# A two-layer transformer trunk on one core: the feed-forward as seven block products on fp32 sums, in two stages with DRAM between them

## The chip, the cores and the metric

The kernel runs on one core of a Trainium2 chip. The metric is device microseconds of one execution. The program uses four compute engines with a queue each, which run in order and wait for each other by semaphores: TensorE (PE: matmuls and transposes into PSUM), VectorE (DVE), ScalarE (ACT) and GpSimd (POOL). SyncE (SP) issues the DMAs. On-chip data lies in SBUF (128 partitions) and in PSUM, whose eight banks hold 128 x 512 fp32 each.

## The reference

The input x has 1024 tokens of 1024 features, all in fp32, and goes through two layers. In short:

```
for layer in range(2):
    mix = mixer(x)                      # layer 0: latent attention and sliding window; layer 1: forgetting and chunked attention
    x = layer_norm(alpha * x + mix, ln1)            # alpha = (2 * 2) ** 0.25
    g = x @ w_gate ; u = x @ w_up                   # 1024 -> 2816
    ffn = (silu(g) * u) @ w_down                    # 2816 -> 1024
    x = layer_norm(alpha * x + ffn, ln2)
```

## The kernel before

**Precision.** TensorE multiplies in a reduced fp32 form (F32R in the code). To keep fp32 accuracy each operand is split in a high part (a cast on ScalarE, L106, or L116 for weights) and a low part (operand minus high part, on VectorE, L107, or for weights on GpSimd, L117). A product is then three matmuls, high by high, high by low and low by high, summed in one PSUM bank (`mm3`, L127). The unit of work is a matmul of 128 x 128 by 128 x 512.

**Order of the work.** The code is written with pools of tiles and handed to a scheduler, which estimates times and puts the instructions of each engine in a fixed queue. What an instruction writes is a tile of a pool (names: g, h, s, t, b and wh/wr in SBUF; pd, ps, pt, pv in PSUM). It can start when the tile's former user is done. So a queue's order is known before the run, and an instruction that waits holds up all that is behind it in its queue.

**One layer.** The mixer writes its heads to DRAM (`o_scr`). `out_proj` reads them back and projects them in two halves of the sum. As each tile of 128 tokens is done, it goes through LN1 in `ln_pipe`: statistics on VectorE (L153), small operations on GpSimd (L144, L146), the normalisation on ScalarE (L163), the gain on GpSimd (L164), the bias on VectorE (L192). `ln_turn` (L172 and the splits at L106 and L107) transposes the tile and puts its high and low parts in `xt`, the transposed activations.

**Feed-forward** (`swiglu_ln`). The 2816 hidden features are 22 tiles f of 128. They are worked through in groups of two (the last of four). For each f, gate and up are computed for two halves of 512 tokens, as `h = silu(g) * u` in 128 features x 1024 tokens. For f = 0 and 1 all is plain: 96 matmuls per f. For f = 2 to 19 the cross terms (high by low, low by high) of part of the sum go through block sums in `gate_up`, in seven instead of eight block products: 90 matmuls. For f = 20 and 21 fewer blocks do so: 92. The sums of weights for this are made by GpSimd (L223). After each group, the group's share of the down product, with each tile's two halves of 512 output features, is added to y in SBUF (L363, L365). In the last group `push` starts LN2 for each tile as it is complete. LN2's transposes (layer 0) feed layer 1. In layer 1, tokens 768 to 1023 of LN2 are normalised by VectorE alone (L200), in halves.

Of the kernel before, what the change touches and what calls it, by code (L numbers as in the profile page):

```python
# [11 lines left out]
F32 = mybir.dt.float32  # L12
# [6 lines left out]
S = 1024  # L19
# [13 lines left out]
CFG = dict(gp=33, wrp=3, whp=5, sp=3, hp=3, bp=2, tp=2, pd=3, ps=2, pt=2, pv=1)  # L33
# [6 lines left out]
class Core:  # L40
# [43 lines left out]
    def t(self, tag="t"):  # L84
        return self.tp.tile([P, 512], F32, tag=tag, bufs=3 if tag == "dt" else 2, name=self.nm("t"))
# [23 lines left out]
    def weight(self, src, cols, hl=None):  # L109
        raw = self.wrp.tile([P, WC], F32, tag="wr", name=self.nm("wr"))[:, 0:cols]  # L110
        if hl is None:
            hl = self.whp.tile([P, 2, WC], F32R, tag="wh", name=self.nm("wh"))
# [12 lines left out]
    def mm3(self, out, stat, mov, first, last):  # L125
        for i, (a, c) in enumerate(((0, 0), (0, 1), (1, 0))):
            self.nc.tensor.matmul(out, stat[a], mov[c], start=first and i == 0, stop=last and i == 2)  # L127
# [50 lines left out]
    def ln_pipe(self, y, g, b, xt, done):  # L178
# [41 lines left out]
    def winograd(self, r, b):  # L220

        for i, (x, z, op) in enumerate(b):
            self.nc.gpsimd.tensor_tensor(r[i], fv(x), fv(r[z] if isinstance(z, int) else z), op=op)  # L223

    def sums_x(self, xt):

        def sums(r, b):
            self.winograd(r, ((b(0, 1), b(0, 0), ALU.subtract), (b(1, 1), 0, ALU.subtract),
                              (b(1, 1), b(0, 1), ALU.subtract), (b(1, 0), 1, ALU.subtract)))

        pair = "p (k c) -> p k c"
# [11 lines left out]
    def sums_w(self, wg, wu, more):
        def sums(r, k):
            self.winograd(r, ((k(wu, 0), k(wu, 1), ALU.add), (r[0], k(wg, 0), ALU.subtract),
                              (k(wg, 0), k(wu, 0), ALU.subtract), (k(wg, 1), 1, ALU.subtract)))

        s = [x for _ in range(2) for x in self.b().bitcast(F32R).rearrange("p (s l c) -> s p l c", s=2, l=2)]
        sums(s, lambda w, i: w[0][:, :, i * 256 : i * 256 + 256])
        r = [[x[:, 0, 0:P], x[:, 1, 0:P], x[:, 0, P:256], x[:, 1, P:256]] for x in s]  # L250
        if more:
            for l, tag in enumerate(("t", "o")):
                e = list(self.t(tag).bitcast(F32R).rearrange("p (s c) -> s p c", s=4))
                sums(e, lambda w, i: w[1][:, l, i * P : i * P + P])
                for i in range(4):
                    r[i].append(e[i])
        return r

    def cross(self, out, w, x, first, last):

        for i, (a, b) in enumerate(zip(w, x)):
            self.nc.tensor.matmul(out, a, b, start=first and i == 0, stop=last and i == len(w) - 1)  # L262

    def gate_up(self, wg, wu, xt, xs, more):


        nc = self.nc
        ss = self.sums_w(wg, wu, more)
        deep = 6 if more else 4
        tiles = ((0, 1, 4), (2, 3, 5))  # L270

        def blk(w, i):
            return [w[k // 4][:, l, k % 4 * P : k % 4 * P + P] for k in tiles[i] if k < deep for l in range(2)]

        def orig(i, half):
            return [self.feat(xt, k, half)[1 - l] for k in tiles[i] if k < deep for l in range(2)]

        def part(w, half, extra):
            p = self.psd()
            for k in range(KT):  # L280
                hl = w[k // 4]
                c = slice((k % 4) * P, (k % 4) * P + P)
                hi, lo = self.feat(xt, k, half)
                for i, (a, x) in enumerate(((0, hi), (0, lo), (1, hi))[0 : 1 if k < deep else 3]):
                    nc.tensor.matmul(p, hl[:, a, c], x, start=k + i == 0, stop=extra is None and k == KT - 1 and i == 2)  # L285
            if extra is not None:
                self.cross(p, *extra, False, True)
            return p

        def single(p, w, x):  # L290
            self.cross(p, w, x, True, True)
            return p
# [947 lines left out]
```

## Time and profile before

| | |
|---|---|
| median of 3 runs | 2534.13 us (2533.58 to 2534.38) |
| profiled execution | 2534.4 us |
| its span in the trace | 2532.6 us |
| mean granted TensorE clock | 0.99 |
| busy: PE, DVE, ACT, POOL | 2452.3, 1358.9, 970.8, 1365.9 us |
| matmul instructions (transposes included) | 12376 |

The span runs from the first to the last instruction in the trace. Busy time is the union of an engine's instructions, including the time in which one is held up after it started. The chain of waits is followed back from the last instruction: its shares tell how much of the span each engine decides. The granted clock is TensorE's clock as a share of its full 2.4 GHz.

### The profile page before, as it was taken

The page shows a single profiled execution, that of the slowest core. Times are in us where ns is not written, and L with a number is a line of the kernel's source. Part 1 is how long each engine was busy: PE and PEld are TensorE (multiplying, and loading weights), DVE is VectorE, ACT ScalarE, POOL GpSimd, SP SyncE. Part 2 cuts the span into 40 slices and gives each one's busy share as a digit, 9 for nine tenths or more (in the row PEclk, how much of TensorE's full clock was granted, in tenths as well). Part 3 has the DMA queues.
Part 4 walks back from the last instruction along what each step waited for, and adds up shares of the span by engine and source line. Part 5 has one row for each costly group of instructions (what it writes and reads, how often), then busy time and mean ns, then how long its engine had stood idle before and what let it go on. Part 6 is the DMA issues. An engine that isn't in the chain of part 4 may idle for free.

```text
span 2532.6 us, 35601 instructions
## 1 busy us (share of the span) xinstructions
PE 2452.3 (97%) x12376; PEld 2067.3 (82%) x12376; DVE 1358.9 (54%) x3096; ACT 970.8 (38%) x2112; POOL 1365.9 (54%) x1604
## 2 busy tenths in 40 slices
PE   8998999999999999999999999999899999999997
PEld 7976888788888888887789898977788888888886
DVE  3477757734444444447356666656724444444447
ACT  5475857422222222223356665555421222222221
POOL 3432545785555555566356553364685555555565
PEclk9999999999999999999999999999999999999999
DMA  4235331111111111112221212142111111111112
GB/s 153 79 101 167 92 119 50 52 51 50 50 50 50 51 50 50 50 55 105 71 78 59 68 45 65 41 154 74 42 44 50 50 51 50 50 50 50 51 57 97
DMA packets 103923, 172.66 MB, mean 68 GB/s; under 512 B 12728, under 2 KB 38712, under 8 KB 103744
## 3 DMA queue, kind: packets, MB, share of 16 engines
q1 hardware_dynamic: 103744, 170.39, 22.5%
q8 instruction: 98, 1.61, 0.3%
q14 instruction: 81, 0.66, 0.1%
HBM read 143.57 MB, written 22.58 MB: 66 GB/s over the span
## 4 chain that ended last, share of the span: by engine, by line
PE 85%; DVE 5%; POOL 3%; DMA 3%; ACT 2%; issue 2%; SPq 0%; POOLq 0%; DVEq 0%; ACTq 0%
PE pd L127 24%; PE ps L127 19%; PE pd L285 17%; PE pd L262 6%; PE pt L262 6%; PE pv L562 4%; PE pt L551 3%; PE pv L262 2%; POOL g L164 1%; PE ps L591 1%; PE ps L592 1%; DVE g L192 1%; DVE m L162 1%; DMA wr<-o_scr 1%; ACT g L163 1%
## 5 line engine op out<-in xcount | busy, mean ns | idle before, releaser
L117 POOL TENSOR_TENSOR wh<-wr,wh 128x512 fp32r<-128x512 f32 (+2 forms) x363 | 482.3, 1337 | 666.9 <-ACT wh L116 637.1
L127 PE MATMUL pd<-g,wh 128*128 128x512 f32 (+1 forms) x2076 | 530.9, 401 | 19.2 <-ACT g L106 10.1
L116 ACT CAST wh<-wr 128x512 fp32r<-128x512 f32 (+2 forms) x363 | 222.2, 613 | 748.6 <-PE pd L285 439.3
L285 PE MATMUL pd<-g,wh 128*128 128x512 f32 x1984 | 501.8, 389 | 0.0
L127 PEld LDWEIGHTS pd<-g,wh 128*128 128x128 f32 (+1 forms) x2076 | 382.7, 189 | 103.8 <-ACT g L106 11.0
L127 PE MATMUL ps<-wh,h 128*128 128x512 f32 x1920 | 460.9, 390 | 1.0 <-DVE g L365 1.0
L285 PEld LDWEIGHTS pd<-g,wh 128*128 128x128 f32 x1984 | 372.4, 188 | 77.3
L127 PEld LDWEIGHTS ps<-wh,h 128*128 128x128 f32 x1920 | 359.5, 188 | 77.4 <-DVE g L365 3.2
L365 DVE TENSOR_TENSOR g<-ps,g 128x512 f32<-128x512 f32 x288 | 197.0, 688 | 320.3 <-PE ps L127 320.3
L534 POOL TENSOR_SCALAR s<-s,m 128x128 f32<-128x128 f32 (+1 forms) x192 | 138.1, 720 | 174.0 <-DVE m L533 147.8
L107 DVE TENSOR_TENSOR h<-pt,h 128x512 fp32r<-128x512 f32 (+3 forms) x318 | 170.0, 543 | 47.3 <-ACT h L106 45.5
L106 ACT CAST h<-pt 128x512 fp32r<-128x512 f32 (+3 forms) x318 | 145.5, 472 | 119.2 <-PE pt L551 111.4
L562 PE MATMUL pv<-h,g 128*128 128x256 f32 x928 | 160.8, 295 | 5.2 <-ACT h L106 4.3
L529 ACT ACTIVATE s<-s,m 128x128 f32<-128x128 f32 (+1 forms) x192 | 143.9, 750 | 43.8 <-DVE m L527 37.7
L127 PE MATMUL pd<-wh,g 128*128 128x256 f32 (+2 forms) x1056 | 158.9, 296 | 0.8 <-DVE t L967 0.6
L127 PEld LDWEIGHTS pd<-wh,g 128*128 128x128 f32 x1056 | 145.2, 194 | 3.5 <-PE pt L939 0.8
L296 DVE TENSOR_TENSOR t<-pd,t 128x512 f32<-128x512 f32 x160 | 106.8, 686 | 72.7 <-PE pd L262 63.3
L562 PEld LDWEIGHTS pv<-h,g 128*128 128x128 f32 x928 | 129.4, 190 | 13.7 <-ACT h L106 6.6
L551 PE MATMUL pt<-ident,s 128*128 128x128 f32 x816 | 133.4, 274 | 6.5 <-DVE h L107 3.8
L296 DVE TENSOR_TENSOR t<-pt,t 128x512 f32<-128x512 f32 x80 | 55.3, 692 | 152.2 <-PE pt L262 150.3
L551 PEld LDWEIGHTS pt<-ident,s 128*128 128x128 f32 x816 | 98.5, 141 | 20.3 <-issue 6.1
L262 PE MATMUL pt<-g,b 128*128 128x512 f32 x320 | 105.0, 389 | 0.0
(192 smaller groups left out, 3798.9 us busy)
## 6 DMA issues: line engine op xcount, KB each, us to landing
wr<-in_wgu SPq DMA_DIRECT2D x176, 256.0 KB, 2.7
wr<-in_wd SPq DMA_DIRECT2D x88, 256.0 KB, 2.6
o_scr<-t SPq DMA_DIRECT2D x128, 64.0 KB, 2.1
wr<-o_scr SPq DMA_DIRECT2D x32, 256.0 KB, 2.8
wr<-in_cd_f SPq DMA_DIRECT2D x32, 256.0 KB, 2.7
s<-in_xT SPq DMA_DIRECT2D x16, 256.0 KB, 5.1
g<-qr_scr SPq DMA_DIRECT2D x32, 128.0 KB, 3.3
g<-kr_scr SPq DMA_DIRECT2D x16, 256.0 KB, 4.2
```

The source lines that it names most:

```text
L106: self.nc.scalar.copy(hi, src)
L107: self.nc.vector.tensor_tensor(lo, src, fv(hi), op=ALU.subtract)
L116: self.nc.scalar.copy(hl[:, 0, :], raw)
L117: self.nc.gpsimd.tensor_tensor(hl[:, 1, :], raw, fv(hl[:, 0, :]), op=ALU.subtract)
L127: self.nc.tensor.matmul(out, stat[a], mov[c], start=first and i == 0, stop=last and i == 2)
L262: self.nc.tensor.matmul(out, a, b, start=first and i == 0, stop=last and i == len(w) - 1)
L285: nc.tensor.matmul(p, hl[:, a, c], x, start=k + i == 0, stop=extra is None and k == KT - 1 and i == 2)
L296: nc.vector.tensor_tensor(o, x, z, op=ALU.add)
L365: nc.vector.tensor_tensor(y[tt][:, o], p, y[tt][:, o], op=ALU.add)
L529: nc.scalar.activation(sb[:, 0:w], sb[:, 0:w], AF.Exp, bias=neg, scale=scale, accum_out=sm)
L551: nc.tensor.transpose(tp[:, (kb - b0) * P : (kb - b0) * P + P], sb[:, (kb - k0) * P : (kb - k0) * P + P], self.ident)
L562: nc.tensor.matmul(pv, vt(kb), pair[kb // 4][:, l, kb % 4, :], start=c == 0, stop=c == 2 * (last + 1 - first) - 1)
```

## The change

**Blocks.** The feed-forward's products are cut in 2 x 2 blocks and computed with seven instead of eight block products (Winograd's form), now on sums of the fp32 values; each sum is split in a high and a low part afterwards, and all three matmuls of a product work on the split sums.

**Gate/up** (`gate_up`). The blocks are the two halves of the tokens, the two halves of the 1024 input features, and gate against up. `turn_sums` takes the place of `ln_turn` after LN1. For tokens 0 to 511 it transposes the tile as before. For tokens 512 to 1023 it makes four sums of 512 columns out of two tiles (two on VectorE, two on GpSimd) and transposes them beside the tile's second half. Per f, four sums of weights are made on GpSimd, and all weights and sums are split by ScalarE and VectorE (`hilo`). One f is 7 x 4 x 3 = 84 matmuls. h is written to DRAM (`h_scr`), and the LN1 output to `xr_scr`.

**Down** (`down`). It runs after all of gate/up. The blocks are the two halves of the tokens, the two halves of the output features, and f = j against f = j + 11. Both h and the weights come from DRAM in one tile of 1024 columns: 512 of h, 512 of weights. The pairs j are worked through in three groups of 3, 4 and 4; y is loaded from `xr_scr` again and multiplied by alpha. A group has seven products on 4 tiles of 128 tokens, and per j 12 matmuls for each product. The sums of h and of weights are made by GpSimd, two by VectorE, each operand is split by ScalarE and VectorE right ahead of its matmuls, and the results are added to y by VectorE and, for u, by GpSimd too.

**Pools.** The h tiles go from three of 2 x 1024 columns to six of 1024, the t tags become one tag with nine tiles, the g pool has 31 instead of 33 tiles, whp six instead of five. In the attention code only the tile names change by this.

```diff
-CFG = dict(gp=33, wrp=3, whp=5, sp=3, hp=3, bp=2, tp=2, pd=3, ps=2, pt=2, pv=1)
+CFG = dict(gp=31, wrp=3, whp=6, sp=3, hp=6, bp=2, tp=9, pd=3, ps=2, pt=2, pv=1)
...
+    def turn_block(self, xb, name, src, tt):
+        p = self.pst()
+        for k in range(4):
+            self.nc.tensor.transpose(p[:, k * P : k * P + P], src[:, k * P : k * P + P], self.ident)
+        o = slice(tt % 4 * P, tt % 4 * P + P)
+        hi, lo = self.block(xb, name)
+        for k in range(2):
+            self.split(hi[k][:, :, o], lo[k][:, :, o], p[:, k * 256 : k * 256 + 256].rearrange("p (k c) -> p k c", k=2))
+    def turn_sums(self, y, xb):
+        nc = self.nc
+        def turn(tt):
+            a, b = slice(0, 512), slice(512, D)
+            if tt < 4:
+                self.turn_block(xb, "b11", y[tt][:, a], tt)
+                self.turn_block(xb, "b21", y[tt][:, b], tt)
+                return
+            x, z = y[tt - 4], y[tt]
+            t1, t2, t3, t4 = (self.t() for _ in range(4))
+            nc.vector.tensor_tensor(t1, z[:, a], x[:, a], op=ALU.subtract)
+            nc.gpsimd.tensor_tensor(t3, z[:, b], z[:, a], op=ALU.subtract)
+            nc.vector.tensor_tensor(t2, z[:, b], t1, op=ALU.subtract)
+            nc.gpsimd.tensor_tensor(t4, x[:, b], t2, op=ALU.subtract)
+            for name, src in (("b22", z[:, b]), ("t1", t1), ("t2", t2), ("t3", t3), ("t4", t4)):
+                self.turn_block(xb, name, src, tt)
+        return turn
...
+    def hilo(self, src, hl):
+        self.split(hl[:, 0], hl[:, 1], src)
+        return hl
...
+        def prep(f):
+            w = {}
+            a11, a21, a22, a12 = (load(wgu[2 * f + i, j]) for i, j in ((0, 0), (1, 0), (1, 1), (0, 1)))
+            st = self.s()
+            sa, sb = st[:, 0:512], st[:, 512:1024]
+            sub = lambda o, x, z: nc.gpsimd.tensor_tensor(o, x, z, op=ALU.subtract)
+            w["a11"] = self.hilo(a11, self.w())
+            nc.gpsimd.tensor_tensor(sa, a21, a22, op=ALU.add)
+            w["s1"] = self.hilo(sa, big())
+            sub(sa, sa, a11)
+            w["s2"] = self.hilo(sa, big())
+            w["a12"] = self.hilo(a12, self.w())
+            sub(sb, a11, a21)
+            w["s3"] = self.hilo(sb, self.h().rearrange("p (l c) -> p l c", l=2))
+            w["a22"] = self.hilo(a22, self.w())
+            sub(sa, a12, sa)
+            w["s4"] = self.hilo(sa, big())
+            return w
...
+        def tail(f, w, u, g):
+            p = self.pst()
+            product(p, w["s3"], "t3")
+            u3 = self.t()
+            nc.vector.tensor_tensor(u3, p, u, op=ALU.add)
+            p5 = self.psd()
+            product(p5, w["s1"], "t1")
+            c22 = self.t()
+            nc.vector.tensor_tensor(c22, p5, u3, op=ALU.add)
+            p = self.pss()
+            product(p, w["a22"], "t4")
+            nc.vector.tensor_tensor(u3, p, u3, op=ALU.add)
+            nc.vector.tensor_tensor(u3, u3, g, op=ALU.mult)
+            nc.sync.dma_start(h_scr[f][:, 0:512], u3)
+            product(p5, w["s4"], "b22", first=False)
+            nc.vector.tensor_tensor(u, p5, u, op=ALU.add)
+            nc.scalar.activation(u, u, AF.Silu)
+            nc.vector.tensor_tensor(c22, c22, u, op=ALU.mult)
+            nc.sync.dma_start(h_scr[f][:, 512:1024], c22)
...
+        for f in range(2, NF):
+            w, nxt = nxt, prep(f + 1) if f + 1 < NF else None
+            p1, u = head(w)
+            m6(w, u)
+            g = gate0(w, p1)
+            tail(f, w, u, g)
...
+    def down(self, y, xr_scr, h_scr, wd, lng, lnb, turn_next, done):
+        nc = self.nc
+        half = NF // 2
+        cuts = (0, 3, 7, half)
+        lo, hi = slice(0, 512), slice(512, 1024)
+        banks = ((self.psd, self.psd, self.psd, self.psv), (self.pss, self.pss, self.pst, self.pst))
...
+        def parts(sides, spare=False):
+            h, l = ((self.g if spare else self.w)() for _ in range(2))
+            if not spare:
+                h, l = (x.rearrange("p s c -> p (s c)") for x in (h, l))
+            for src, o in sides:
+                self.split(h[:, o], l[:, o], src)
+            return h, l
+        def mms(p, op, mt, first, last, more=False):
+            h, l = op
+            c = slice(mt * P, mt * P + P)
+            self.mm3(p, (h[:, c], l[:, c]), (h[:, hi], l[:, hi]), first, last, more)
+        def product(p, n, sides, first=True):
+            for j in range(n):
+                op = parts(sides(j))
+                for mt in range(4):
+                    mms(p[mt], op, mt, first and j == 0, j == n - 1, not first)
+        add = lambda e, o, x, z: e.tensor_tensor(o, x, z, op=ALU.add)
+        sub = lambda e, o, x, z: e.tensor_tensor(o, x, z, op=ALU.subtract)
+        push = None
+        for j0, j1 in zip(cuts[:-1], cuts[1:]):
+            n = j1 - j0
+            last = j1 == half
+            ld = [load(j) for j in range(j0, j1)]
+            r11, r21, r22, r12 = ([ld[j][i]() for j in range(n)] for i in (0, 2, 3, 1))
+            if j0 == 0:
+                for tt in range(TT):
+                    y[tt] = self.g(F32)
+                    nc.sync.dma_start(y[tt], xr_scr[tt * P : tt * P + P, :])
+                    nc.scalar.mul(y[tt], y[tt], ALPHA)
...
+                push = self.ln_pipe(y, self.load_row_bcast(lng), self.load_row_bcast(lnb), turn_next, done)
+            both = lambda r: lambda j: ((r[j], slice(0, 1024)),)
+            p1 = bank()
+            product(p1, n, both(r11))
+            us = [self.s() for _ in range(2)]
+            u = [us[mt // 2][:, mt % 2 * 512 : mt % 2 * 512 + 512] for mt in range(4)]
+            for mt in range(4):
+                nc.scalar.copy(u[mt], p1[mt])
+            x = [self.h(F32) for _ in range(n)]
+            for j in range(n):
+                add(nc.gpsimd, x[j][:, lo], r21[j][:, lo], r22[j][:, lo])
+                sub(nc.gpsimd, x[j][:, hi], r21[j][:, hi], r11[j][:, hi])
+            p5 = bank()
+            product(p5, n, both(x))
+            for mt in range(4):
+                add(nc.vector, y[4 + mt][:, hi], p5[mt], y[4 + mt][:, hi])
+            product(p1, n, both(r12), first=False)
+            for mt in range(4):
+                add(nc.vector, y[mt][:, lo], p1[mt], y[mt][:, lo])
+            for j in range(n):
+                sub(nc.gpsimd, x[j][:, lo], x[j][:, lo], r11[j][:, lo])
+                sub(nc.gpsimd, x[j][:, hi], r22[j][:, hi], x[j][:, hi])
+                sub(nc.gpsimd, r12[j], r12[j], x[j])
+            product(p5, n, lambda j: ((r12[j][:, lo], lo), (r22[j][:, hi], hi)), first=False)
+            for mt in range(4):
+                add(nc.vector, y[mt][:, hi], p5[mt], y[mt][:, hi])
+            p = bank()
+            product(p, n, both(x))
+            for mt in range(4):
+                add(nc.vector, u[mt], p[mt], u[mt])
+                add(nc.gpsimd, y[mt][:, hi], u[mt], y[mt][:, hi])
+                if last:
+                    push(mt)
+            for j in range(n):
+                sub(nc.vector, r21[j][:, lo], r11[j][:, lo], r21[j][:, lo])
+                sub(nc.vector, r21[j][:, hi], r22[j][:, hi], r21[j][:, hi])
+            p = bank()
+            product(p, n, both(r21))
+            for mt in range(4):
+                add(nc.vector, u[mt], p[mt], u[mt])
+                add(nc.gpsimd, y[4 + mt][:, hi], u[mt], y[4 + mt][:, hi])
+                add(nc.gpsimd, y[4 + mt][:, lo], u[mt], y[4 + mt][:, lo])
+            sides = lambda j: ((r22[j][:, lo], lo), (r12[j][:, hi], hi))
+            p = bank()
+            if last:
+                ops = [parts(sides(j), True) for j in range(n)]
+                for mt in range(4):
+                    for j in range(n):
+                        mms(p[mt], ops[j], mt, j == 0, j == n - 1)
+                    add(nc.vector, y[4 + mt][:, lo], p[mt], y[4 + mt][:, lo])
+                    push(4 + mt)
+            else:
+                product(p, n, sides)
+                for mt in range(4):
+                    add(nc.vector, y[4 + mt][:, lo], p[mt], y[4 + mt][:, lo])
         return push
...
-        push = c.ln_pipe(y, lng, lnb, xt, lambda tt, yt, o=None: None)
+        push = c.ln_pipe(y, lng, lnb, c.turn_sums(y, xb), lambda tt, yt, xr_scr=xr_scr: nc.sync.dma_start(xr_scr[tt * P : tt * P + P, :], yt))
```

The queues change as follows. First GpSimd's queue inside the feed-forward of layer 0; before, these rows make the low parts (wh from wr, its weights as loaded) and sums (b, t) of a pair of f, in gate/up:

```order
L117 TENSOR_TENSOR wh_1643_7371<-wr_1642_7370,wh_1643_7371 128x512
L117 TENSOR_TENSOR wh_1645_7376<-wr_1644_7375,wh_1645_7376 128x512
L117 TENSOR_TENSOR wh_1647_7381<-wr_1646_7380,wh_1647_7381 128x512
L117 TENSOR_TENSOR wh_1649_7386<-wr_1648_7385,wh_1649_7386 128x512
L223 TENSOR_TENSOR b_1651_7391<-wh_1647_7381 128x512
L223 TENSOR_TENSOR b_1652_7392<-wh_1643_7371,wh_1647_7381 128x512
L223 TENSOR_TENSOR t_1653_7397<-wh_1649_7386 128x128
L223 TENSOR_TENSOR t_1653_7397<-wh_1645_7376,wh_1649_7386 128x128
L223 TENSOR_TENSOR t_1654_7402<-wh_1649_7386 128x128
L223 TENSOR_TENSOR t_1654_7402<-wh_1645_7376,wh_1649_7386 128x128
L117 TENSOR_TENSOR wh_1671_7530<-wr_1670_7529,wh_1671_7530 128x512
L223 TENSOR_TENSOR b_1651_7391<-b_1651_7391,wh_1643_7371 128x512
```

After, in the first group of down (x sums in h_2080 to h_2082, r12 in g_2057 to g_2059; h_2165 to h_2167 are the x sums of the second group):

```order
L432 TENSOR_TENSOR h_2081_9752<-h_2081_9752,g_2049_9636 128x512
L432 TENSOR_TENSOR h_2081_9752<-g_2055_9654,h_2081_9752 128x512
L432 TENSOR_TENSOR h_2082_9753<-h_2082_9753,g_2050_9639 128x512
L432 TENSOR_TENSOR h_2082_9753<-g_2056_9657,h_2082_9753 128x512
L432 TENSOR_TENSOR h_2165_10249<-g_2139_10139,g_2135_10127 128x512
L432 TENSOR_TENSOR g_2057_9660<-g_2057_9660,h_2080_9751 128x1024
L432 TENSOR_TENSOR g_2058_9663<-g_2058_9663,h_2081_9752 128x1024
L431 TENSOR_TENSOR h_2165_10249<-g_2139_10139,g_2143_10151 128x512
L432 TENSOR_TENSOR h_2166_10250<-g_2140_10142,g_2136_10130 128x512
L431 TENSOR_TENSOR h_2166_10250<-g_2140_10142,g_2144_10154 128x512
L432 TENSOR_TENSOR h_2167_10251<-g_2141_10145,g_2137_10133 128x512
L432 TENSOR_TENSOR g_2059_9666<-g_2059_9666,h_2082_9753 128x1024
```

GpSimd's weight lows are gone. Sums for the next group now stand between the second and third subtraction from r12 (the rows with 128x1024), on which the fourth product of this group works.

Second, TensorE's queue at the end of layer 0's feed-forward. Before, `ps` are down products of one token tile and one half of the features (all their matmuls together), and `pt` the transposes of LN2's tiles (g_1092 is token tile 0, g_1093 tile 1):

```order
L127 MATMUL ps_2323_11277<-wh_2292_11114,g_2264_10962 128x512 x2
L127 MATMUL ps_2323_11277<-wh_2292_11114,g_2265_10963 128x512
L172 MATMUL pt_2321_11259<-ident_99,g_1092_4754 128x128 x4
L172 MATMUL pt_2322_11268<-ident_99,g_1092_4754 128x128 x4
L127 MATMUL ps_2324_11291<-wh_2294_11119,h_2182_10493 128x512 x3
L127 MATMUL ps_2324_11291<-g_2295_11123,h_2210_10652 128x512 x3
L127 MATMUL ps_2324_11291<-g_2297_11128,h_2238_10811 128x512 x3
L127 MATMUL ps_2324_11291<-g_2299_11133,g_2264_10962 128x512 x2
L127 MATMUL ps_2324_11291<-g_2299_11133,g_2265_10963 128x512
L127 MATMUL ps_2332_11338<-wh_2286_11099,h_2182_10493 128x512 x3
L127 MATMUL ps_2332_11338<-wh_2288_11104,h_2210_10652 128x512 x3
```

After, ps_2348 and ps_2349 are two of the four token tiles of the sixth product of the last group, g_2060 and g_2061 are token tiles 0 and 1 of y, and pd_2360 belongs to the seventh, last product:

```order
L127 MATMUL ps_2348_11287<-wh_2356_11323,wh_2357_11324 128x512
L127 MATMUL ps_2349_11288<-wh_2357_11324,wh_2356_11323 128x512
L127 MATMUL ps_2349_11288<-wh_2356_11323,wh_2357_11324 128x512
L172 MATMUL pt_2339_11226<-ident_99,g_2060_9669 128x128 x4
L172 MATMUL pt_2340_11235<-ident_99,g_2060_9669 128x128 x4
L172 MATMUL pt_2346_11261<-ident_99,g_2061_9672 128x128 x4
L172 MATMUL pt_2347_11270<-ident_99,g_2061_9672 128x128 x4
L127 MATMUL pd_2360_11367<-g_2364_11371 128x512
L127 MATMUL pd_2361_11368<-g_2364_11371 128x512
```

Before, 24 matmuls stand between the transposes of tile 0 and the first of tile 1. After, all four transposes stand together, in front of the seventh product (pd_2360 to pv_2363) and of the sixth's other two token tiles (pt_2350 and pt_2351).

## Rows read from the trace of the kernel before

**Rows 1.** The page: busy time by engine; the chain that ended last, by engine.

```profile
PE 2452.3 (97%) x12376; PEld 2067.3 (82%) x12376; DVE 1358.9 (54%) x3096; ACT 970.8 (38%) x2112; POOL 1365.9 (54%) x1604
...
PE 85%; DVE 5%; POOL 3%; DMA 3%; ACT 2%; issue 2%; SPq 0%; POOLq 0%; DVEq 0%; ACTq 0%
```

**Rows 2.** Windows: stretch, length; busy by engine; granted clock, DMA share, GB/s.

```profile
700.00:750.00 50.00, 50.00 (x223) 41.40 (x222) 25.08 (x36) 11.62 (x19) 28.38 (x27) 1.00 0.20 59
465.00:505.00 40.00, 35.46 (x166) 28.59 (x165) 32.33 (x53) 16.61 (x30) 25.80 (x21) 0.96 0.11 31
1775.00:1830.00 55.00, 47.13 (x206) 37.84 (x205) 41.68 (x65) 19.82 (x33) 36.76 (x30) 0.91 0.13 34
1165.00:1240.00 75.00, 71.46 (x338) 52.76 (x336) 46.31 (x85) 28.69 (x57) 40.54 (x33) 0.98 0.27 92
```

**Rows 3.** Timeline, TensorE and VectorE's last: start, duration, [idle before, its releaser].

```profile
492.39 1.00 PE L172 MATMUL pt<-ident,g 128*128 128x128 f32 x4 [3.72 <-DVE g L107]
493.04 4.80 PE L127 MATMUL pd<-g,wh 128*128 128x512 f32 x14
...
879.82 2.88 PE L127 MATMUL ps<-wh,h 128*128 128x512 f32 x12
882.54 0.39 PE L262 MATMUL pt<-s,b 128*128 128x512 f32 x1
...
1175.52 0.60 PE L172 MATMUL pt<-ident,g 128*128 128x128 f32 x4
1175.88 0.95 PE L127 MATMUL ps<-wh,h 128*128 128x512 f32 x3
...
2518.83 0.84 PE L127 MATMUL ps<-g,g 128*128 128x512 f32 x3
...
2528.06 1.41 DVE L200 SCALAR_TENSOR_TENSOR g<-g,m,b 128x512 f32<-128x512 f32 x2 [0.44 <-POOL m L146]
```

**Rows 4.** Timeline of GpSimd and VectorE in a gate/up stretch of layer 0.

```profile
869.51 1.29 POOL L117 TENSOR_TENSOR wh<-wr,wh 128x512 fp32r<-128x512 f32 x1
869.59 0.69 DVE L365 TENSOR_TENSOR g<-ps,g 128x512 f32<-128x512 f32 x1 [0.67 <-PE ps L127]
870.88 1.29 POOL L223 TENSOR_TENSOR b<-wh 128x512 fp32r<-128x512 f32 x1
872.13 1.29 POOL L223 TENSOR_TENSOR b<-wh,wh 128x512 fp32r<-128x512 f32 x1
...
891.73 1.29 POOL L117 TENSOR_TENSOR wh<-wr,wh 128x512 fp32r<-128x512 f32 x1 [8.06 <-ACT wh L116]
892.31 1.26 DVE L301 TENSOR_TENSOR t<-t,t 128x512 f32<-128x512 f32 x1
893.91 4.31 POOL L117 TENSOR_TENSOR wh<-wr,wh 128x512 fp32r<-128x512 f32 x3 [0.89 <-ACT wh L116]
895.13 0.68 DVE L107 TENSOR_TENSOR h<-t,h 128x512 fp32r<-128x512 f32 x1
```

**Rows 5.** Timeline of GpSimd and VectorE in LN2 of layer 1.

```profile
2488.49 2.39 POOL L164 TENSOR_TENSOR g<-g,b 128x1024 f32<-128x1024 f32 x1
2492.14 1.21 DVE L192 TENSOR_TENSOR g<-g,b 128x1024 f32<-128x1024 f32 x1
2492.25 3.36 POOL L164 TENSOR_TENSOR g<-g,b 128x1024 f32<-128x1024 f32 x1 [1.37 <-ACT g L163]
```

**Rows 6.** Groups by line and form: busy us, mean ns; idle before, releasers.

```profile
L365 DVE TENSOR_TENSOR g<-ps,g 128x512 f32<-128x512 f32 x288 | 197.0, 688 | 320.3 <-PE ps L127 320.3
L107 DVE TENSOR_TENSOR g<-pt,g 128x256 fp32r<-128x256 f32 x100 | 40.4, 417 | 30.2 <-ACT g L106 29.3
L163 ACT ACTIVATE g<-g,m,m 128x1024 f32<-128x1024 f32 x30 | 37.2, 1244 | 89.8 <-DVE m L162 89.7
```

**Rows 7.** A window of 5 us with heavy DMA traffic; columns as in rows 2.

```profile
1665.00:1670.00 5.00, 5.00 (x27) 4.24 (x26) 2.52 (x10) 1.90 (x4) 3.11 (x4) 1.00 1.04 411
```

**Rows 8.** The page's DMA issues: count, KB each, median us to landing.

```profile
wr<-in_wgu SPq DMA_DIRECT2D x176, 256.0 KB, 2.7
```

More of the change, by code (lines that the diff above doesn't have):

```diff
@@ L111, in weight @@
         if hl is None:
-            hl = self.whp.tile([P, 2, WC], F32R, tag="wh", name=self.nm("wh"))
+            hl = self.w()
         hl = hl[:, :, 0:cols]
@@ L123, in ftile, with mm3 @@
         return [self.weight(src[i], 512, tile()) for i in range(2)]
-    def mm3(self, out, stat, mov, first, last):
+    def mm3(self, out, stat, mov, first, last, more=False):
         for i, (a, c) in enumerate(((0, 0), (0, 1), (1, 0))):
-            self.nc.tensor.matmul(out, stat[a], mov[c], start=first and i == 0, stop=last and i == 2)
+            self.nc.tensor.matmul(out, stat[a], mov[c], start=first and i == 0, stop=last and i == 2, skip_group_check=more)
     def fproj(self, ws, xt, half):
@@ L243, in sums_w @@
[L243 to L264, printed above, removed]
-        nc = self.nc
[L268 to L292, printed above, removed]
-        def add(x, z, tag):
-            o = self.t(tag)
-            nc.vector.tensor_tensor(o, x, z, op=ALU.add)
-            return o
-        def gated(g, u):
-            nc.scalar.activation(g, g, AF.Silu)
-            nc.vector.tensor_tensor(u, u, g, op=ALU.mult)
-            return u
-        m1 = self.t("dt")
-        nc.scalar.copy(m1, single(self.psv(), blk(wg, 0), orig(0, 0)))
-        g0 = add(part(wg, 0, (blk(wg, 1), orig(1, 0))), m1, "t")
-        c21 = part(wu, 0, (blk(wu, 1), xs[3]))
-        u2 = add(single(self.pst(), ss[1], xs[1]), m1, "dt")
-        u3 = add(single(self.pst(), ss[2], xs[2]), u2, "dt")
-        yield gated(g0, add(c21, u3, "o"))
-        m5 = single(self.pst(), ss[0], xs[0])
-        nc.vector.tensor_tensor(u2, m5, u2, op=ALU.add)
-        nc.vector.tensor_tensor(u3, m5, u3, op=ALU.add)
-        g1 = add(part(wg, 1, (ss[3], orig(1, 1))), u2, "t")
-        yield gated(g1, add(part(wu, 1, None), u3, "o"))
@@ new lines, in blocks, with block @@
+    def blocks(self):
+        make = lambda h: [[(self.h if h else self.g)().rearrange("p (k c) -> p k c", k=2) for _ in range(2)] for _ in range(2)]
+        return {}, make
+    def block(self, xb, name):
+        blk, make = xb
+        if name not in blk:
+            blk[name] = make(name == "b22")
+        return blk[name]
+    def turn_block(self, xb, name, src, tt):
[6 more added lines that the diff above has]
+            self.split(hi[k][:, :, o], lo[k][:, :, o], p[:, k * 256 : k * 256 + 256].rearrange("p (k c) -> p k c", k=2))
@@ L539, in t @@
                 if g not in pair:
-                    pair[g] = self.h().rearrange("p l (k q) -> p l k q", q=256)
+                    pair[g] = [self.h().rearrange("p (k q) -> p k q", q=256) for _ in range(2)]
                 b0, b1 = max(4 * g, k0), min(4 * g + 4, i + 1)
```

219 lines of the change are left out of this document (117 added, 102 removed).

## The prediction

> **What bounds the kernel now.** First the busy shares and the chain of waits. TensorE is busy 2452.3 us of a span of 2532.6, 97%, and holds 85% of the chain; VectorE, ScalarE and GpSimd are at 54, 38 and 54% [rows 1]. So time is matmul columns plus the few places where TensorE waits. Then one stretch inside the feed-forward: in 50 us TensorE is busy 50.00 at a granted clock of 1.00, with VectorE at 25.08 and GpSimd at 28.38 [rows 2]. There nothing but the number of matmuls counts. Next the stretches in which TensorE isn't full [rows 2]. From the first layer norm of layer 0 into its feed-forward (465 to 505 us) it is busy 35.46 of 40 at a clock of 0.96: 4.5 us idle and about 0.04 x 40 = 1.6 lost to the clock, 6. The same place in layer 1 (1775 to 1830): 7.9 idle and 0.09 x 55 = 5.0, 13. End of layer 0's feed-forward (1165 to 1240): 3.5 and 1.5, 5. After the last matmul, which ends at 2518.83 + 0.84 = 2519.7 [rows 3], come 12.9 us of layer norm and output. The profiled execution took 2534.4, 1.8 more than its span; the median of the runs is 2534.1.
>
> **Durations.** Twelve 128x512 matmuls begin at 879.82 and what follows begins at 882.54: 2.72/12 = 0.227 us each. Four 128x128 transposes take 1175.88 - 1175.52 = 0.36, 0.09 each [rows 3]. GpSimd on 512 columns starts at 870.88 and 872.13, so 1.25 [rows 4]; on 1024 it shows 2.39 [rows 5], so some 2.36. VectorE on 1024 columns from SBUF shows 1.21 [rows 5], some 1.17 without overlap, so 0.6 for 512; reading PSUM it shows 0.69 [rows 6].
>
> **Port.** VectorE with two operands in SBUF and GpSimd run one after the other. GpSimd's subtract starts at 891.73 and takes 1.29; VectorE's multiply starts within it, at 892.31, and shows 1.26, over twice the 0.6 of such an operation. Three GpSimd subtracts take 4.31 instead of 3.75 while VectorE splits 512 columns at 895.13 [rows 4]. With 1024 columns, VectorE starts at 2492.14 and takes 1.21; GpSimd starts 0.11 later and shows 3.36 instead of 2.39, longer by about what was left of VectorE's [rows 5]. A VectorE operation on PSUM beside GpSimd's subtract at 869.51 keeps its 0.69 [rows 4]. I therefore add the times of GpSimd and of VectorE's two-SBUF operations as if on one engine.
>
> The Trainium skill ("SBUF — State Buffer", Who interferes with whom) says the same: VectorE with two SBUF inputs contends with GpSimd's reads, and of the shared port pair the first to issue holds it for its whole instruction. The trace agrees, with the 3.36 against 2.39 above. It speaks against this change, which moves weight lows from GpSimd to VectorE and adds GpSimd sums. Without that rule the down stage below would cost nothing and the forecast would be 40 us lower.
>
> **The change, part by part.**
>
> Matmuls. Before, a layer has 2 x 96 + 18 x 90 + 2 x 92 = 1996 in gate/up and 22 x 8 x 2 x 3 = 1056 in down. After, 22 x 7 x 4 x 3 = 1848, and 11 x 7 x 4 x 3 = 924. That is 280 fewer a layer, 560 in all: 560 x 0.2267 = -126.9 us. All stood on the path.
>
> Transposes. The block sums after LN1 are turned too: 112 instead of 64 a layer, 96 x 0.0885 = +8.5.
>
> Gate/up, steady. One f is 84 matmuls, 19.0 us. VectorE has 9 two-SBUF operations (5.4) and 5 on PSUM (3.4), GpSimd 4 sums (5.0): 10.4 of shared port in 19.0, and the next f is prepared a whole f ahead. Cost 0. Four 256 KB loads (2.7 us each [rows 8]) and two stores fit in 19 us. If the cover went, 10.4 us would have to be exposed per f; nothing suggests it.
>
> LN1 into gate/up. For tokens 512 to 1023, each of four tiles makes four sums and five transposed, split blocks. From order and rows: VectorE 41 splits of 256 columns (0.417 shown, on PSUM [rows 6]) 16, 22 two-SBUF operations of 512 13, 4 bias adds 4.6, evacuations and statistics 5: 39 us. GpSimd has 18 x 1.25 + 3 x 2.36 = 30 beside them, and I let 9 of it delay VectorE: 48. TensorE has 83 matmuls and 80 transposes, 26, in that stretch. So about 22 us idle, against 6 and 13 before: +16 and +9, +25. Bounds: no delay at the port, 13 idle (+7 and 0); the 30 in full, 43 idle (+37, +30).
>
> Gate/up to down. The down stage reads what gate/up stored. Group 0 loads 24 blocks of 256 KB, and 4 MB of y; a stretch loading at 411 GB/s [rows 7] makes that some 25 us, most of it beside the last f. I take +1.5 a layer, +3; 0 to 16.
>
> Down. A group of n pairs is 84n matmuls: 76.2 us for 4, 57.1 for 3. Port time for 4: VectorE 28 splits of 1024 (32.8) and 8 subtracts of 512 (4.8); GpSimd 4 x (4 x 1.25 + 2.36) = 29.4 and 12 adds of 512 (15.0): 82.0. For 3 it is 65.3. A layer has 82.0 + 82.0 + 65.3 = 229.3 of port under 209.4 of matmuls: +20 a layer, +40. Below, if the port's work starts before the stage and runs past it, 0. Above: in each group the second product needs the x sums, 10 us of GpSimd, in a queue with 12 adds; exposed in all three groups, 30 a layer, +60. I take +40, the sum itself. GpSimd's queue speaks for it: in group 0 sums for group 1 stand ahead of the last r12 difference on which group 0's fourth product waits.
>
> End of layer 0. TensorE's queue has the transposes of LN2 for tokens 0 to 255 in front of half of the last group's sixth product and all of its seventh. LN2 of a tile goes through GpSimd (four adds of 1.25, four small operations, one multiply of 2.36), ScalarE 1.24 [rows 6] and VectorE, some 28 us with the port's waits for the first two tiles; TensorE has 66 matmuls (15 us) to cover it. Then eight more adds (10) stand between the sixth product and the second half's LN2, with layer 1's projections on half 0 as cover. I take 25 idle in all against 5 before: +20; 0 to +40.
>
> End of layer 1. The seventh product (10.9 us of matmuls) starts when the sixth is done; in GpSimd's queue then stand eight adds (10.0) and two LN multiplies (4.7), so they end 4.8 behind the last matmul, then 8 small operations (6), ScalarE 1.2, two multiplies (4.7), VectorE's last add (1.2) and the 3.1 that now lie between VectorE's last end, 2529.47 [rows 3], and the span's: 21, with waits at the port 24. Against 12.9: +11; +3 to +18.
>
> Clock. After the 3.72 us wait of before, 14 matmuls took 4.80 instead of 3.17 [rows 3]. A few more waits of that length in each layer: +6; 0 to +15.
>
> Attention. Queue orders differ only locally: 0, +-5.
>
> Sum: -126.9 + 8.5 + 25 + 3 + 40 + 20 + 11 + 6 = -13.4. Profiled 2534.4 gives 2521.0, the median 2520.7: **2521**.
>
> **Rivals.** A, the waits pack away: splits and sums of down run ahead during products, VectorE's PSUM work fills what the port leaves, and transposes find their tile ready. For it: GpSimd and VectorE are each near half load, and before shows stretches of TensorE at 50.00 of 50. Against it: the port sum of 229 over 209. With down +10, LN1 +13, end +10, tail +9, transition 3, clock 4: -118.4 + 49 = -69, 2465. Chance 0.25.
>
> B, slower: in the down stage each product's first split waits at the port behind a GpSimd instruction and queues behind PSUM evacuations, and PSUM has only two banks of four products, so evacuations that stand behind a waiting split hold up the next product. Price 2.36 + 1.2 + 4 x 0.69 = 6.3 us at each product start, half covered: 3.2; 21 products a layer, 67, instead of 20: +94, 2615 in full; at half of that excess 2568. It decides from 18 us over forecast: 0.4 us a product. For it: VectorE does the split of the operand directly before its matmuls, in order. Against: the whp pool holds three split operands ahead. Chance 0.27.
>
> C, no gain in matmuls because products end up waiting for h through DRAM: loads land in 2.7 us [rows 8] and are issued a group ahead; in A's and the forecast's spread.
>
> **How the numbers follow.** The forecast has 0.48 with 2500 to 2545 as its own range; A 0.25, B 0.27. A measurement of this kernel tells no more than 0.2%, 5 us. Of the forecast's 0.48, 0.32 lie below 2529, 0.10 within 5 us, 0.06 above; B leaves 0.02 within. Faster 0.57, same 0.12, slower 0.31. The range reaches to A's 2465 and to B at half, 2578 with its spread.
>
> **What would show it.** Gate/up: windows with TensorE full and 19.0 us an f. Down: windows with GpSimd's and VectorE's two-SBUF work together near the window's length and TensorE at 90 to 92%; at 99% A holds, below 85% B. LN1: about 22 us idle at each layer. Layer 0's end: TensorE waiting at the transposes of the first two tiles. Tail: 24 us. The forecast is wrong if down's TensorE share lies outside 88 to 95%, or if an f takes over 20 us.

## The result, and the profile after

The change made the kernel slower: 2607.2 us (median of 4 runs, 2601.2 to 2610.0) against 2533.9 (median of 4 runs), ratio 1.0286 [1.0266, 1.0306]. The forecast was 2521, with a range from 2465 to 2578. The profiled execution took 2609.2 us, 74.8 more than that of before.

The page of the changed kernel, busy time by engine and the clock in 40 slices:

```profile
PE 2400.5 (92%) x11912; PEld 2000.6 (77%) x11912; DVE 1692.0 (65%) x3346; ACT 1140.0 (44%) x2358; POOL 1183.8 (45%) x1346
...
PEclk9999999889999999998899999999889999999998
```

TensorE has 464 instructions fewer than in [rows 1] (560 matmuls less, 96 transposes more), yet its busy time fell by 52 us only, where they are worth 118. And its idle time rose from 80.3 to 206.9 us. The windows say where (columns as in [rows 2]): LN1 of layer 0, gate/up, down, the end of layer 0, LN1 of layer 1, down of layer 1, the tail.

```profile
470.00:560.00 90.00, 65.77 (x283) 51.69 (x284) 68.39 (x119) 38.76 (x84) 50.28 (x38) 0.79 0.29 100
560.00:950.00 390.00, 390.00 (x1724) 323.04 (x1723) 210.67 (x287) 114.79 (x198) 100.32 (x77) 1.00 0.30 92
950.00:1176.00 226.00, 204.90 (x859) 164.07 (x858) 193.51 (x176) 87.76 (x108) 145.13 (x81) 0.97 0.30 105
1176.00:1276.00 100.00, 71.12 (x291) 53.21 (x291) 66.81 (x99) 35.91 (x66) 57.03 (x47) 0.80 0.18 65
1838.00:1930.00 92.00, 63.85 (x267) 49.15 (x266) 71.04 (x117) 38.79 (x83) 48.73 (x38) 0.80 0.31 100
2326.00:2578.00 252.00, 228.49 (x947) 181.37 (x945) 216.33 (x211) 98.29 (x121) 159.51 (x93) 0.96 0.25 90
2578.00:2607.40 29.40, 0.00 (x0) 0.00 (x0) 24.22 (x28) 2.37 (x2) 21.54 (x17) 0.59 0.29 116
```

Gate/up is full, at a clock of 1.00, and a tile f takes 19.0 us. The other stretches have gaps, and around the gaps a lower clock. To tell the two apart I cut the span in windows of 2 us and summed, in each, the idle time and busy time x (1 - granted clock). The second is the busy time that the same work would not have needed at full clock ("slow clock" below). It says where TensorE's time lies; it does not say that the kernel would be shorter by as much, since an engine that is sooner done can wait longer. Before, gate/up and down alternate, so their row is the whole feed-forward between its two ends:

| us | idle before | idle after | slow clock before | slow clock after |
|---|---|---|---|---|
| LN1 into gate/up, both layers | 12.6 | 52.4 | 6.2 | 25.4 |
| down, both layers (before: with gate/up) | 3.2 | 44.6 | 0 | 14.6 |
| end of layer 0 | 3.3 | 28.9 | 1.7 | 10.9 |
| tail | 12.9 | 29.4 | 0 | 0 |
| the rest | 48.3 | 51.6 | 10.3 | 13.3 |
| sum | 80.3 | 206.9 | 18.2 | 64.2 |

So -118.4 (work) + 126.6 (idle) + 46.0 (slow clock) = 54 of the 75 us. The other 21 us are in no column. The matmul ahead of a wait shows 0.39 us instead of 0.227, and TensorE has 79 gaps in the feed-forward and at its ends instead of 20: an estimate of 10 us. Some us more lie in the attention: the 2485 matmuls and transposes ahead of LN1 of layer 0 take 470 us instead of 464, with the same idle time (32.0 and 32.6) and only 3.4 more of slow clock. I did not split the rest, and why the attention got longer stays open.

The clock in LN1 of layer 0, in three waits and three windows of 4 us:

```profile
498.39 1.08 PE L236 MATMUL pt<-ident,g 128*128 128x128 f32 x4 [5.61 <-DVE g L106]
501.88 1.09 PE L236 MATMUL pt<-ident,g 128*128 128x128 f32 x4 [2.40 <-DVE g L106]
502.61 6.09 PE L127 MATMUL pd<-g,wh 128*128 128x512 f32 x14
...
536.83 1.94 PE L236 MATMUL pt<-ident,t 128*128 128x128 f32 x8 [5.68 <-DVE g L106]
```

```profile
540.00:544.00 4.00, 1.94 (x8) 1.57 (x8) 2.32 (x6) 1.48 (x5) 2.52 (x2) 0.50 0.28 74
548.00:552.00 4.00, 4.00 (x11) 3.12 (x10) 1.83 (x5) 1.00 (x2) 1.28 (x1) 0.50 0.47 131
552.00:556.00 4.00, 4.00 (x23) 3.42 (x22) 0.44 (x2) 0.74 (x2) 1.29 (x1) 0.98 0.00 0
```

After waits of 5.61 and 2.40 us, 14 matmuls take 6.09 us instead of 3.17. Through the waits around 540 the granted clock is 0.50, 1.2 GHz. From 548 to 552 TensorE is busy 4.00 of 4 us and still at 0.50: the window has 11 matmuls, cut-off ones included, where 4 us at full clock have room for 17. From 552 the clock is back.

What TensorE waits for at LN1, on three engines in order of time:

```profile
541.29 1.94 PE L236 MATMUL pt<-ident,t 128*128 128x128 f32 x8 [2.52 <-DVE g L106]
...
542.41 0.37 ACT L105 CAST g<-pt 128x256 fp32r<-128x256 f32 x1 [1.20 <-PE pt L236]
543.27 0.65 ACT L105 CAST g<-pt 128x256 fp32r<-128x256 f32 x2 [0.48 <-PE pt L236]
...
542.82 0.42 DVE L106 TENSOR_TENSOR g<-pt,g 128x256 fp32r<-128x256 f32 x1 [1.14 <-ACT g L105]
543.67 0.76 DVE L106 TENSOR_TENSOR g<-pt,g 128x256 fp32r<-128x256 f32 x2 [0.43 <-ACT g L105]
```

I read this as a ring: transposes fill a bank (pt, two of them), ScalarE casts, VectorE subtracts, and only then the bank takes the next transposes. All three wait for each other. In down it looks different, here in the second group (in order: TensorE, VectorE, GpSimd):

```profile
1073.34 1.24 PE L127 MATMUL ps<-wh,wh 128*128 128x512 f32 x4 [3.07 <-DVE wh L106]
...
1058.61 1.77 DVE L432 TENSOR_TENSOR g<-g,g 128x512 f32<-128x512 f32 x1
1060.30 2.31 DVE L106 TENSOR_TENSOR wh<-g,wh 128x1024 fp32r<-128x1024 f32 x1
1069.92 3.37 DVE L106 TENSOR_TENSOR wh<-g,wh 128x1024 fp32r<-128x1024 f32 x1
...
1059.79 1.74 POOL L432 TENSOR_TENSOR h<-g,h 128x512 f32<-128x512 f32 x1
1063.72 8.48 POOL L432 TENSOR_TENSOR g<-g,h 128x1024 f32<-128x1024 f32 x3
```

VectorE has no gaps, but each operation is stretched: 3.37 us for 1024 columns that take 1.21 alone [rows 5]. GpSimd's three take 8.48 instead of 7.1. Here TensorE's wait ends with VectorE's split of 3.37 us. At the end of layer 0 TensorE stands at the transposes of LN2, as the queue ahead of the prediction shows:

```profile
1194.20 1.97 PE L172 MATMUL pt<-ident,g 128*128 128x128 f32 x8 [10.30 <-DVE g L192]
...
1179.02 6.00 POOL L431 TENSOR_TENSOR g<-s,g 128x512 f32<-128x512 f32 x4 [11.24 <-DVE s L431]
1188.41 11.23 POOL L164 TENSOR_TENSOR g<-g,b 128x1024 f32<-128x1024 f32 x4
```

### The profile page after: what moved, and what is told of

It reads as the page before. It is cut to its first block, busy times and chain, and to the rows that moved or that the text cites. A ratio compares the mean times of both kernels' runs of the same rounds, so it can differ in the third digit from the quotient of the medians.

```text
span 2607.4 us, 35582 instructions
## 1 busy us (share of the span) xinstructions
PE 2400.5 (92%) x11912; PEld 2000.6 (77%) x11912; DVE 1692.0 (65%) x3346; ACT 1140.0 (44%) x2358; POOL 1183.8 (45%) x1346
## 5 line engine op out<-in xcount | busy, mean ns | idle before, releaser
L127 PE MATMUL pd<-g,wh 128*128 128x512 f32 (+1 forms) x2940 | 757.2, 403 | 19.5 <-ACT g L105 7.6
L127 PEld LDWEIGHTS pd<-g,wh 128*128 128x128 f32 (+1 forms) x2940 | 553.2, 192 | 145.4 <-ACT g L105 8.7
L106 DVE TENSOR_TENSOR wh<-g,wh 128x512 fp32r<-128x512 f32 (+1 forms) x138 | 201.5, 1498 | 32.8 <-ACT wh L105 23.8
L106 DVE TENSOR_TENSOR h<-pt,h 128x512 fp32r<-128x512 f32 (+2 forms) x334 | 176.3, 537 | 51.7 <-ACT h L105 49.9
L116 POOL TENSOR_TENSOR wh<-wr,wh 128x512 fp32r<-128x512 f32 (+4 forms) x113 | 139.0, 1238 | 152.1 <-ACT wh L115 109.0
L105 ACT CAST h<-pt 128x512 fp32r<-128x512 f32 (+2 forms) x334 | 150.6, 467 | 126.7 <-PE pt L691 115.0
L127 PE MATMUL ps<-g,g 128*128 128x512 f32 (+3 forms) x816 | 197.7, 378 | 6.3 <-DMA g<-kr_scr 4.6
L127 PE MATMUL pd<-g,g 128*128 128x512 f32 (+2 forms) x768 | 176.9, 374 | 1.4 <-ACT g L105 1.4
L127 PEld LDWEIGHTS ps<-g,g 128*128 128x128 f32 x816 | 146.2, 189 | 33.3 <-DVE m L663 4.0
L127 PEld LDWEIGHTS pd<-g,g 128*128 128x128 f32 x768 | 138.9, 189 | 24.8 <-ACT g L105 2.2
```

The costliest lines, as they stand in the source:

```text
L105: self.nc.scalar.copy(hi, src)
L106: self.nc.vector.tensor_tensor(lo, src, fv(hi), op=ALU.subtract)
L116: self.nc.gpsimd.tensor_tensor(hl[:, 1, :], raw, fv(hl[:, 0, :]), op=ALU.subtract)
```

## The experiments

The theory after these rows: down waits for the port (the access to SBUF by which the prediction has VectorE's two-SBUF operations and GpSimd run one after the other), LN1 for the port and VectorE's work, the end and the tail for the order of LN2, and the slow clock follows the waits. The rivals: down waits for DRAM or for late splits; LN1 for its two banks; the clock falls by itself. All numbers of idle and slow clock are made as in the table above.

**Down as before, gate/up as changed.** `down` gives way to the loop of the kernel before, with h loaded from DRAM:

```diff
-            product(p1, n, both(r11))
...
+                raw = self.s()
+                nc.sync.dma_start(raw, h_scr[f])
+                self.split(h, l, raw)
...
+                    self.mm3(p, (hs[i][0][:, tt * P : tt * P + P], hs[i][1][:, tt * P : tt * P + P]),
+                             (ds[n][i][:, 0], ds[n][i][:, 1]), i == 0, i == c1 - c0 - 1)
```

> The changed gate/up is kept; the down product goes back to eight block products per group of two f (the last of four), without sums, with h read from DRAM and split there. It has 132 more matmuls a layer than the change, 60 us in all. Theory (the 44 us of idle in down, 25 at the end of layer 0, 16 at the tail and about 37 us of slow clock behind them belong to down's sums, splits and order): all of these go and about 2545 us, with TensorE over 97% busy in down. Rival (reading h and the LN1 output back through DRAM is what makes down wait): down keeps 40 us or more of waits and the 60 us are added, 2600 to 2665.

Measured 2582.8 us. End of layer 0 and tail are near those of the kernel before (4.4 and 11.3 idle). Down keeps 23 us idle. Its largest waits, in the list of TensorE's waits (us in total, times, longest):

```profile
PE ps L127 <- DVE g L420: 13.5, 21, 1.4
...
PE ps L127 <- ACT h L105: 5.1, 2, 3.2
```

The first is PSUM's evacuation on VectorE, which now also splits h; of the large ones only the second, the first cast of h in each layer, can hide a load. LN1 is unchanged (52.2 idle). So neither number came. The rival wanted 40 us of waits for DRAM, and these rows leave it some 5. With down's sums and their order 64 us of idle and 17 of slow clock go, for 60 of matmuls; the run does not tell sums and order apart.

**All sums on VectorE.**

```diff
-            sub = lambda o, x, z: nc.gpsimd.tensor_tensor(o, x, z, op=ALU.subtract)
+            sub = lambda o, x, z: nc.vector.tensor_tensor(o, x, z, op=ALU.subtract)
...
-                add(nc.gpsimd, x[j][:, lo], r21[j][:, lo], r22[j][:, lo])
+                add(nc.vector, x[j][:, lo], r21[j][:, lo], r22[j][:, lo])
```

(and so at all sums of tokens, weights and blocks and the u adds)

> All two-SBUF sums and adds of the feed-forward that the change gave to GpSimd run on VectorE instead (token sums, weight sums, block sums and u adds of down). Theory (GpSimd and VectorE's two-SBUF work exclude each other, so 512 columns cost 1.25 of the shared port on GpSimd and 0.6 on VectorE): port time of a down group of four falls from 82 to about 60 us, VectorE with its PSUM work to about 76; idle in down falls from 44 to about 20 us and at LN1 from 51 to about 40, the slow clock with it: about 2560 us. Rival (the engines don't hold each other up; down waits for late splits in VectorE's queue): VectorE gets 20 us more per group and its queue is later: 2620 to 2650.

Measured 2572.0 us. Windows of down in layer 0 and of LN1:

```profile
940.00:1160.00 220.00, 213.21 (x916) 171.81 (x915) 194.83 (x264) 91.19 (x112) 0.82 (x4) 0.99 0.33 120
468.00:556.00 88.00, 63.86 (x278) 49.54 (x277) 73.59 (x140) 37.92 (x84) 23.49 (x18) 0.79 0.29 102
```

In down GpSimd's busy time went from 145.13 to 0.82 us and VectorE's stayed at 194, with 88 operations more: the time it had spent waiting was as long as the work it took over. Down's idle fell from 44.6 to 15.6, its slow clock from 14.6 to 3.2. The end of layer 0 and the tail did not gain: their idle rose to 34.5 and 32.5 us, so that the u adds run on GpSimd is not what makes them long. At LN1 the idle time did not fall either (55.2 us, expected 40): GpSimd's sums do not set that stretch, and that half of the theory falls. LN1's gain (L164) stayed on GpSimd, and VectorE got more work there, so a smaller share of the port is not excluded.

**Unused sums on GpSimd.** To the run before, five sums per pair in down that nobody reads:

```diff
+                for _ in range(5):
+                    add(nc.gpsimd, self.t(), r21[j][:, lo], r22[j][:, lo])
```

> The run with all sums on VectorE, and GpSimd makes five more sums of 512 columns per pair in down that nobody reads (55 a layer, 69 us of GpSimd). Theory (exclusion at the port): nobody waits for them and yet down's idle rises from 16 to about 60 us, the slow clock with it: 2615 to 2635 us. Rival (sums on VectorE were better only because each is done sooner, 0.6 instead of 1.25): 2572, within 6.

Measured 2648.6 us, 77 more than without them, and more than expected. GpSimd's sums in layer 0, VectorE's beside them and, from 1024 on, behind them, and the window of down:

```profile
989.35 25.84 POOL L431 TENSOR_TENSOR t<-g,g 128x512 f32<-128x512 f32 x14
...
1000.04 1.75 DVE L432 TENSOR_TENSOR h<-g,g 128x512 f32<-128x512 f32 x1
...
1024.66 0.67 DVE L431 TENSOR_TENSOR h<-g,g 128x512 f32<-128x512 f32 x1
...
1003.50 1.22 PE L127 MATMUL ps<-wh,wh 128*128 128x512 f32 x2 [5.11 <-DVE wh L106]
```

```profile
950.00:1190.00 240.00, 207.29 (x832) 163.47 (x832) 231.07 (x251) 86.38 (x107) 98.01 (x59) 0.92 0.27 97
```

In the list of waits no wait of VectorE or TensorE in down ends on these sums, and yet VectorE's beside them take 1.75 us, and 0.67 once GpSimd is done. Down's idle rose from 15.6 to 66.9 us. This is the two engines holding each other up, as on one port, and not lateness of a sum.

**Five banks for the transposes after LN1.**

```diff
-        p = self.pst()
+        self.tb = getattr(self, "tb", 0) + 1
+        p = (self.pst, self.pst, self.pss, self.pss, self.psv)[self.tb % 5]()
```

> The transposes after LN1 go round five PSUM banks instead of two; nothing else. Theory A (the LN1 waits are a chain of transpose, cast, subtract, and bank free again, with two banks): idle there falls from 51 us in both layers to about 30, the slow clock by 15: about 2575 us. Theory B (VectorE's amount of work and its waits at the port set the stretch): 2600 to 2610, idle unchanged.

Measured 2560.5 us, better than theory A's number; B, as what sets the stretch, falls. LN1 of layer 0:

```profile
468.00:556.00 88.00, 77.32 (x365) 62.12 (x364) 78.75 (x134) 41.25 (x90) 56.16 (x42) 0.92 0.34 114
```

LN1's idle fell from 52.4 to 24.5 and the slow clock from 25.4 to 8.6; down stayed at 47.7. VectorE's busy time rose: it had been waiting too.

**Waits filled with matmuls.**

```diff
+        if tt >= 4:
+            x = self.block(xb, "b11")[0]
+            q = self.psv()
+            for k in range(4):
+                self.nc.tensor.matmul(q, x[0][:, 0, o], x[k // 2][:, k % 2], start=k == 0, stop=k == 3)
```

> Behind each transposed block of tokens 512 to 1023 after LN1, TensorE does four more 128x512 matmuls whose result is not used (20 blocks a layer, 80 matmuls, 18 us at full clock). Theory (the granted clock falls because TensorE waits, and matmuls after a wait run at the lower level): the clock in the two LN1 stretches rises from 0.64 to 0.95 to near 1.00, the 18 us of slow clock a layer go, the extra matmuls lie mostly in waits: 2580 to 2600 us. Rival (the lower clock does not come from the waits): the clock there stays, and the extra matmuls add 18 us or more a layer: 2640 to 2660.

Measured 2600.6 us, just above the expected range. LN1 of layer 0:

```profile
468.00:560.00 92.00, 80.95 (x381) 63.99 (x381) 69.53 (x124) 40.46 (x86) 52.12 (x39) 0.93 0.29 99
```

160 matmuls (36 us) were added, and the kernel became no slower. The clock in the stretch rose from 0.79 to 0.93, the slow clock at LN1 fell from 25.4 to 9.7 us (the expectation had it too large, at 18 a layer), and idle from 52.4 to 24.5. So the clock falls because TensorE waits. But the kernel gained 7 us only: 15.7 us of slow clock and 28 of idle time went, and 36 us of extra work took their place. From LN1's first transpose to its last it takes 84 and 90 us instead of 91 and 95.

**Together.** Five banks, and x and r12 on VectorE with the u adds left on GpSimd:

> The five banks of the run before for the transposes, and in down the sums of blocks (x, r12) on VectorE; the adds of u to y stay on GpSimd, as in the change. Theory (LN1 is a chain through two banks, down is the shared port, and the two don't touch each other): LN1 as with five banks alone (25 us idle in both layers), down as with all sums on VectorE (45 us idle becomes 10 to 15, slow clock 10 us less): 2515 to 2522 us, under the kernel before. Rival (the u adds on GpSimd still hold VectorE up): down keeps 30 us idle, about 2540.

Measured 2529.9 us, ratio to the kernel before 0.998 [0.9969, 0.9991]: 8 us above the expected range. The two cures nearly add up (2607 - 47 - 35 = 2525). LN1 has 26 us idle as expected, down 20 instead of 10 to 15; that the u adds on GpSimd are the difference is not shown. Then the last four f as before, tile by tile (cuts 0, 3, 6, 9):

> The run with five banks and block sums on VectorE, and in addition only nine of eleven pairs (three groups of three) go through seven products; the last four f are added with eight products tile by tile, as in the kernel before, so that LN2 runs from tile to tile. 24 more matmuls a layer, 11 us in all. Theory (the end of layer 0, 28 us idle and 9 of slow clock, and 15 of the 28 us tail come from the order in which the seven products complete the tiles): 46 us go, 11 come: about 2482 us. Rival (LN2 itself, its work and its engines, is what takes long there): end and tail stay within 5 us and the 11 are added, about 2530.

Measured 2514.7 us, 0.9917 [0.9899, 0.9934], 33 above the theory's number. The end of layer 0 has 4 us idle (28 with five banks alone), the tail 11 instead of 29; but down got worse (19 us idle in layer 0 instead of 9), and the rows at a group's start show the largest new wait:

```profile
995.84 12.17 POOL L432 TENSOR_TENSOR g<-s,g 128x512 f32<-128x512 f32 x8 [3.10 <-DVE s L432]
...
1003.47 1.74 DVE L433 TENSOR_TENSOR g<-g,g 128x512 f32<-128x512 f32 x1
...
1006.94 2.93 PE L127 MATMUL pd<-wh,wh 128*128 128x512 f32 x6 [5.69 <-DVE wh L106]
```

Eight u adds in a row on GpSimd hold up VectorE's sums and splits, on which the next group waits (VectorE also waited 1.8 us for a load of h there). At the start of the last four f TensorE waits 4.9 us more, for the low parts of their weights, which stand behind eight such adds in GpSimd's queue. So the u adds went to VectorE too, and with them these low parts:

> The run with the last four f tile by tile, and now the u adds of down and the low parts of the last four f's weights on VectorE too, so that GpSimd has nothing left in down. Theory (eight adds in a row on GpSimd at a group's end, 12 us at the port, hold up the sums and splits with which the next group starts, 12 us idle and 7 of slow clock in layer 0 and as much in layer 1): 2495 to 2502 us. Rival (VectorE is full with groups of three: 63 us of work by 57 of matmuls): the gain is eaten, 2512 to 2525.

Measured 2495.1 us, 0.9846 [0.983, 0.9863], as expected; which of the two moves gave how much was not tested. Last, `cuts = (0, 4, 9)`:

> As the run with everything on VectorE in down, but the nine pairs in two groups of four and five instead of three of three: the adds and evacuations, 24 us of VectorE a group, come twice instead of three times, so VectorE has 164 us a layer where TensorE has 171 (three groups: 188). Theory (VectorE's sum decides): 2485 to 2495 us. Rival (a group of five holds 20 of 23 tiles, so the blocks of the second group are loaded and summed too late): 10 us or more idle at its start in each layer, 2500 to 2515.

Measured 2479.1 us, 0.9778 [0.9764, 0.9793]: 2.2% faster than the kernel before, and 6 us below the expected range. The rival's wait at the second group's start is there, at 4.8 us idle in layer 0 instead of 10 or more. Down of layer 0 and the page:

```profile
920.00:1136.00 216.00, 209.14 (x893) 168.28 (x892) 183.20 (x250) 88.42 (x112) 4.90 (x5) 0.98 0.33 120
```

```profile
PE 2367.4 (96%) x11960; PEld 1981.4 (80%) x11960; DVE 1616.9 (65%) x3448; ACT 1118.8 (45%) x2338; POOL 867.7 (35%) x1164
```

## Why the prediction was wrong

The profiled time came out 88.2 us above the forecast. By the table, 40.0 of them are the slow clock (46.0 where 6 were set), 27.6 are idle time (126.6 where the terms had 99), and 20.6 are in no term. The matmuls and gate/up came out as worked out, down's idle time too, and neither of the two signs that were to prove the forecast wrong appeared (TensorE's share in down is 91%, an f takes 19.0 us): none of them looked at the clock.

The step that failed is "Clock. [...] A few more waits of that length in each layer: +6; 0 to +15." The slow clock is 46 us more than before, three times the upper bound. I had counted waits by their number and priced the one of [rows 3] at 1.6 us; in the changed kernel waits follow each other so closely that TensorE stays at the low level, at LN1 of layer 0 for 10 to 17 us on end, and what it does in them takes about twice as long (6.09 us for 14 matmuls). And I set the new idle time against the old idle and the old slow clock together, which gave back 8 us that were not to be had. The second error is the mechanism at LN1, where engines were added up that wait for each other. Term by term:

- Matmuls and transposes, -126.9 and +8.5: the counts are right, and an f takes 19.0 us as worked out.
- LN1, +25: 44 us idle were expected and 52.4 came, 40 more than before. That 44 was so near is in part luck, because the mechanism was wrong: not VectorE's amount of work with GpSimd's at the port (moving GpSimd's sums away left 55) but a ring through two banks (five halve it, to 24.5). I had added up engines and left out that each waits for the other. What the 24.5 wait for was not tested.
- Down with its transition, +43: idle rose by 41.4, and TensorE's share was 91%. That VectorE and GpSimd hold each other up here is shown by two runs, one that takes GpSimd's work away and one that adds unused work; 15.6 us of idle are left without GpSimd's sums.
- End of layer 0, +20: idle rose by 25.6. Tail, +11: by 16.5. The order in which the tiles get ready for LN2 is the likely cause: the run that restores it has 4 and 11 us idle there. That run also takes the last four f out of the seven products, so the order alone is not shown; that it is not GpSimd's u adds is shown (34.5 and 32.5 us idle with them on VectorE).
- Attention, 0: idle +3, slow clock +3, and in layer 0 alone 6 us in all, outside the +-5 that were set for both layers.

Rival B had the right side but not the way: it wanted 67 us a layer of port waits in down, and there were 22. Rival A needed waits to pack away; they did not in this kernel. Only with five banks, the sums on VectorE, two groups and the last four f plain does the time, 2479, come near A's 2465.

## What to carry to other kernels

A plan that saves matmuls but opens waits must be priced twice: the wait, and the matmuls behind it at half clock, as long as waits keep coming (46 us here, beside 127 of idle). A sum with two operands in SBUF costs GpSimd twice VectorE's time (1.25 us against 0.6 for 512 columns) and holds up VectorE's two-SBUF operations meanwhile, so look first at what VectorE does beside it. Before adding up an engine's work, look for rings through a pool of two.

## What the hardware showed that was not expected

GpSimd's 110 unused sums, on which no engine waits in down, took 195.8 us instead of 110 x 1.25 = 138 and made the kernel 77 us longer: both engines lose. And matmuls put into waits came free: with 36 us of them at LN1 the time was 7 us below the changed kernel's median. They lie in what was idle time before, and the clock in the stretch rose from 0.79 to 0.93.

```profile
L431 POOL TENSOR_TENSOR t<-g,g 128x512 f32<-128x512 f32 x110 | 195.8, 1815 | 1035.1 <-DMA g<-h 1034.5 <-DVE t L363 0.6
```
